# Convolution inputs and half of the pre-normed activations in PSUM, and a smaller fill for two column tiles

## The chip, the cores and the metric

The kernel runs on one core of a Trainium2 chip. The metric is the device time of one execution in microseconds. The core's engines are named as in the profile: PE is TensorE (PEld its weight loads), DVE is VectorE, ACT is ScalarE, POOL is GpSimd, SP the engine that issues most of the weight DMAs. SBUF is the working memory; PSUM is the accumulation memory that the matmuls write, here used as eight banks of 128 x 512 f32.

## What is computed

One inference step of a four-layer decoder trunk with model width 1024, for a prompt of 512 positions and a sample group of 8 sequences with 4 new positions each. Every layer is a token mixer followed by a SwiGLU feed-forward network, each behind an RMS norm and with a residual. Only the second mixer matters here, the Conformer convolution:

```python
z = einsum(h, w_in) + b_in;  a, gate = split(z)
g = a * sigmoid(gate)
ext = concatenate([buf, g])                  # buf: the last 30 rows (zeros for the prompt)
c = depthwise_causal(ext, dw) + dw_b         # 31 taps per channel
c = silu(layernorm(c));  y = einsum(c, w_out)
```

For a sample sequence `ext` has 30 + 4 rows, and each of its four outputs is the sum of 31 products per channel.

## The kernel before

**Tiling.** Channels lie on the 128 partitions; a width of 1024 is NC = 8 column tiles. The positions are two halves: A holds 256 prompt positions, B the other 256 and the 32 sample positions (8 sequences by 4). Every f32 product is three matmuls of split operands (hi by hi, hi by lo, lo by hi). The "hi" copy of weights and activations is an ACT cast, the "lo" part is a subtraction of two SBUF operands on DVE or POOL.

**The order of the work.** `Stream` (L258) holds a list of steps: each has weight loads, matmuls (`mm`, L393, or `mm_pair`, L413) and an evacuation generator. Python writes the program of every engine in order, and each engine runs its own in order. `Timed` (L91) adds up an estimated time for DVE (`dve.t`), POOL and PE while the program is written. Side work, such as the taps of the convolution, is a generator put on a job list; after each step `background` (L287) takes pieces of it until `dve.t` has reached `pe.t - MARGIN[fill]`. `MARGIN` (L1553) is -1.0 for fill 0, 2, 4 and 0.5 for fill 1, 3, 5: with the first, DVE's program is filled to 1.0 us past PE's estimated time, with the second to 0.5 us short of it.

**Weights** come by SP's DMA into four "raw" buffers, are cast by ACT into "hi" and subtracted into "lo"; where `rel` is set, as in the stretch of this case, POOL does most of the "lo" parts (`Load.low`, L171).

**The stages around the change** (us from the span's start): conv_in(A), 224 to 280; ffn(0, B), 280 to 491, with the taps of half A as background; the output projection of A, 491 to 516; conv_in(B), 516 to 572; ffn(1, A), 572 to 774, with the taps of half B, and behind them its layer norm, as background.

**Pre-normed activations.** `Norm.prepare` (L543) multiplies x by gain and 1/rms before the matmuls, for half B of layer 0's FFN (nf0), half B of conv_in (n1) and half A of layer 1's FFN (nf1). For each pair of column tiles DVE writes `hn_` (L552), ACT casts it to `H_h_`, and `split_lo` (L611) subtracts: the odd tile of the pair on DVE, the even one on POOL.

**The convolution.** For each column tile c, `gate_evac` (L1076) makes the sigmoid, `a_evac` (L1104) writes `ce_` (prompt) and `cs_` (sample: 8 x 34 columns, 30 from the state's DMA) and starts the job `conv_taps` (L1157). The job runs 31 taps over 256 prompt positions into two PSUM accumulators `ct0` and `ct1` and then, for half B, the sample positions two at a time: one DVE multiply of overlapping windows of `cs_` by the taps (SBUF by SBUF, 2 x 8 x 31 = 496 elements) into a PSUM tile `cw_`, and one DVE reduce of it to 16 elements. The taps' operand, a slice of `colsT`, has its 31 values 8 f32 apart. `conv_norm` (L1205) follows the last tile.

PSUM tiles all come from one pool of eight (`PS`, L126); a new tile waits for the last use of the tile whose bank it takes. SBUF tiles of this size (`T`, L123) come from a pool of 104.

Of the kernel before, what the change touches and what calls it, by code (L numbers as in the profile page):

```python
# [12 lines left out]
ALU = mybir.AluOpType  # L13
PSUM = bass.MemoryType.PSUM

P = 128
D = 1024
NC = D // P
SEQ = 512
DB, DS = 8, 4  # L20
# [9 lines left out]
CW, SW = 31, 3  # L30
# [8 lines left out]
HP = SEQ // 2  # L39
# [14 lines left out]
C_DW = C_CB + 2 * NC  # L54
# [17 lines left out]
def trunk_kernel(  # L72
# [11 lines left out]
    ap = ctx.enter_context(tc.tile_pool(name="ap", bufs=NBUF))  # L84
# [4 lines left out]
    act = nc.scalar  # L89
# [29 lines left out]
    dve = Timed(nc.vector, operand, 0.00104, 0.07, LEAST)  # L119
# [3 lines left out]
    def T(name, dt=F32):  # L123
        return ap.tile([P, TW], dt, tag="A", name=name)

    def PS(name):  # L126
        return pp.tile([P, 512], F32, tag="ps", name=name)

    def b3(v, n=DB):
        return v.rearrange("p (b l) -> p b l", b=n)  # L130

    x = [cp.tile([P, NC, HW[h]], F32, tag=f"x{h}", name=f"x{h}") for h in (A, B)]
    colsT = cp.tile([P, N_COL], F32, tag="par", name="colsT")
# [9 lines left out]
    def col(i):  # L143
        return colsT[:, i : i + 1]
# [233 lines left out]
    def settle(most=9):  # L378


        t = max(dve.t, pool.t) + SETTLE
        while pe.t < t and most and not S.draining:
            most -= 1
            yield None
# [116 lines left out]
    class Norm:  # L501
# [41 lines left out]
        def prepare(self, h, eng):  # L543
            w, nm = HW[h], f"{self.name}_{h}"
            yield
            out = yield from token_rsqrt(self.acc, (h,), nm, settle(RLAG))
            r = out[h]
            yield
            for c in range(0, NC, 2):
                vs = []  # L550
                for i in (c, c + 1):
                    v = T(f"hn_{nm}_{i}")[:, :w]  # L552
                    dve.scalar_tensor_tensor(
                        v, x[h][:, i, :], gains[:, self.g + i : self.g + i + 1], r[:, :w],
                        op0=ALU.mult, op1=ALU.mult,
                    )
                    self.hs[h][i] = split(v, w, f"h_{nm}_{i}")
                    vs.append(v)
                yield
                for i, v in zip((c, c + 1), vs):  # L560
                    split_lo(self.hs[h][i], v, w, dve if i % 2 else eng)
# [42 lines left out]
    def split(src, w, name):  # L604

        hi = T(f"H_{name}", F32R)
        lo = T(f"L_{name}", F32R)
        act.copy(hi[:, :w], src)  # L608
        return hi, lo

    def split_lo(parts, src, w, eng):  # L611
        hi, lo = parts
        eng.tensor_sub(lo[:, :w], src, hi[:, :w].bitcast(F32))
# [5 lines left out]
    def cols_of(src, name, share, sum=False):  # L619

        return [Load(src[:, i], 1024, f"{name}_{i}", share, sum) for i in range(2)]
# [255 lines left out]
    t = wp.tile([P, 1024], F32, tag="hi", name="ht_0", bufs=AHI + 1)  # L877
# [192 lines left out]
    LS = CB + DS  # L1070

    def conv_in(h, fill):
        w = HW[h]
        sig, exts = {}, {}

        def gate_evac(ps, c):  # L1076
            yield from n1.wait((h,))
            t = sig[c] = T(f"ct_{h}_{c}")
            src = ps[h]
            if h not in n1.pre:  # L1080
                dve.tensor_mul(t[:, :w], ps[h][:, :w], n1.r[h][:, :w])
                src = t
            act.activation(t[:, :w], src[:, :w], AF.Sigmoid, bias=col(C_CB + NC + c))
            yield

        def a_mm(wt, c):
            e = ext[h][c] = T(f"ce_{h}_{c}")
            if h == A:
                pool.memset(e[:, :CB], 0.0)
            else:  # L1090
                pool.tensor_copy(e[:, :CB], cpre[:, c, :])
            if wt:
                return mm(wt, n1.hs, (h,), f"ca_{c}")

        def gate_mm(wt, c, ps=None):
            if h == B:
                for cc in ((0, 1) if c == 0 else (c + 1,)):
                    if cc < NC:
                        exts[cc] = T(f"cs_{cc}")
                        nc.sync.dma_start(exts[cc][:, : DB * LS], st_conv[cc])  # L1100
            ps = ps or mm(wt, n1.hs, (h,), f"cg_{c}")
            return n1.first(ps, (h,)) if c == 0 else ps

        def a_evac(ps, c):  # L1104
            yield from n1.wait((h,))
            e = ext[h][c]
            t = sig.pop(c)
            q = ps[h]
            if h not in n1.pre:
                q = T(f"cq_{h}_{c}")  # L1110
                dve.tensor_mul(q[:, :w], ps[h][:, :w], n1.r[h][:, :w])
            ba = col(C_CB + c)
            ev = None
            if h == B:
                ev = b3(exts[c][:, : DB * LS])
                dve.scalar_tensor_tensor(
                    ev[:, :, CB:], b3(q[:, HP:w]), ba, b3(t[:, HP:w]), op0=ALU.add, op1=ALU.mult
                )
            dve.scalar_tensor_tensor(
                e[:, CB : CB + HP], q[:, :HP], ba, t[:, :HP], op0=ALU.add, op1=ALU.mult  # L1120
            )
            if h == A:
                pool.tensor_copy(cpre[:, c, :], e[:, HP : HP + CB])
            else:
                nc.sync.dma_start(o_cp[:, c, :], e[:, HP : HP + CB])
                nc.sync.dma_start(o_cs[:, c], ev[:, :, DS:])
            S.job(conv_taps(h, c, e, ev))
            if c == NC - 1:
                S.job(conv_norm(h))
            yield  # L1130

        def pair_mm(wt):
            pss = mm_pair((wt[:NC], wt[NC:]), n1.hs, (h,), "cga")
            a_mm(None, 0)
            gate_mm(None, 0, pss[0])
            return pss

        for c in range(NC):
            la, lg = cols_of(w_cin[c], f"ci{c}_{h}", True)
            if c == 0:  # L1140
                S.add([lg, la], pair_mm, lambda pss: both(gate_evac(pss[0], 0), a_evac(pss[1], 0)),
                      flush=True, fill=fill)
                continue
            S.add([lg], lambda wt, c=c: gate_mm(wt, c),
                  lambda ps, c=c: gate_evac(ps, c), flush=(c == 0), fill=fill)
            S.add([la], lambda wt, c=c: a_mm(wt, c), lambda ps, c=c: a_evac(ps, c),
                  fill=fill)

    late = []

    def windows(ev, t):

        v = ev[:, :, t : t + CW]
        p, b, k = v.ap
        return bass.AP(tensor=v.tensor, offset=v.offset, ap=[p, [1, 2], b, k])

    def conv_taps(h, c, e, ev):  # L1157
        w = HW[h]
        cc = cv[h][c] = T(f"cc_{h}_{c}")

        outs = [PS(f"ct{i}_{h}_{c}")[:, :HP] for i in range(2)]
        for k in range(CW):
            o = outs[k % 2]
            wk = col(C_DW + k * NC + c)
            src = e[:, k : k + HP]
            if k == 0:
                dve.tensor_scalar(o, src, wk, col(C_DWB + c), op0=ALU.mult, op1=ALU.add)
            elif k == 1:
                dve.tensor_scalar(o, src, wk, None, op0=ALU.mult)
            else:  # L1170
                dve.scalar_tensor_tensor(
                    cc[:, :HP] if k == CW - 1 else o, src, wk, o, op0=ALU.mult, op1=ALU.add
                )
            if k == 11 and late:
                late.pop()()
            if k % 2:
                yield 0.8
        if ev is not None:

            taps = colsT[:, C_DW + c : C_DW + CW * NC : NC].unsqueeze(1).unsqueeze(1).to_broadcast([P, 2, DB, CW])  # L1180
            for t in range(0, DS, 2):
                pr = PS(f"cw_{c}_{t}")
                pv = pr[:, : 2 * DB * CW].rearrange("p (i b k) -> p i b k", i=2, b=DB)
                dve.tensor_mul(pv, windows(ev, t), taps)
                dve.tensor_reduce(
                    b3(cc[:, HP:w]).rearrange("p b t -> p t b")[:, t : t + 2, :],
                    pv,
                    axis=mybir.AxisListType.X, op=ALU.add,
                )
                yield 1.2  # L1190
            pool.tensor_scalar(cc[:, HP:w], cc[:, HP:w], col(C_DWB + c), None, op0=ALU.add)
        dve.tensor_add(cc[:, :HP], cc[:, :HP], outs[1])

        def gather():

            if c == 0:
                accm[h] = T(f"cm_{h}")
                act.copy(accm[h][:, :w], cc[:, :w])
            else:
                pool.tensor_add(accm[h][:, :w], accm[h][:, :w], cc[:, :w])  # L1200

        late.append(gather)
        yield 0.7
# [291 lines left out]
    for c in range(NC):  # L1495
        lc, lx = cols_of(w_sin[c], f"si{c}", 0)
        S.add([lc], lambda wt, c=c: cg_mm(wt, c),
              lambda ps, c=c: cg_evac(ps, c), flush=(c == 0))
# [175 lines left out]
```

## Time and profile before

| what | us |
|---|---|
| median of 3 runs | 2146.82 |
| lowest, highest of them | 2145.12, 2147.32 |
| the profiled execution, its own time | 2145.55 |
| its span, first to last instruction | 2143.8 |
| mean granted PE clock, share of full speed | 0.993 |

The profile covers one execution. Its busy times say how long an engine executed; a wait row says which engine waited before which operation, for whom, and for how long in total. The time that counts is the median of the runs; the profiled execution is 1.27 us below it.

### The profile page before, as it was taken

Reading aid. Unit: us, or ns where it says so; the run is one execution under the profiler, and the core shown is the slowest. Engines: PE = TensorE matmul, PEld = TensorE weight load, DVE = VectorE, ACT = ScalarE, POOL = GpSimd, SP = SyncE. Lnnn points to the kernel's source line nnn. Section 1 sums busy time; section 2 is a strip of 40 time slices with the busy share of each in tenths; the row PEclk is TensorE's granted clock in tenths of the full one; section 3 lists DMA queues with packets and bytes.
Section 4 is the critical chain, followed back from the end, with each engine's and each line's share of the span. In section 5 each row is a group of like instructions: output and inputs, shape, how many; then the busy total and the mean of one; then the engine's idle time right before and its main releaser. Section 6 shows DMA issues by size and latency. Waiting matters only on the chain.

```text
span 2143.8 us, 42353 instructions
## 1 busy us (share of the span) xinstructions
PE 2107.1 (98%) x16678; PEld 2096.1 (98%) x16678; DVE 1500.7 (70%) x3159; ACT 1017.0 (47%) x1770; POOL 651.4 (30%) x502
## 2 busy tenths in 40 slices
PE   9999999999999999999999999999999999999997
PEld 9999999999999999999999999999999999999997
DVE  8857799616999666566488667686765649585675
ACT  5445543535444654344335646364532246364463
POOL 4011687879788840000043102021000001011121
PEclk9999999999999999999999999999999999999998
DMA  7645555556856564546224746565545555575562
GB/s 270 201 143 168 182 182 148 177 155 181 171 167 187 158 206 152 172 160 179 96 82 141 170 114 153 133 147 145 136 97 87 94 140 109 133 163 126 138 151 72
DMA packets 130191, 320.81 MB, mean 150 GB/s; under 512 B 32557, under 2 KB 40329, under 8 KB 129729
## 3 DMA queue, kind: packets, MB, share of 16 engines
q1 hardware_dynamic: 110664, 279.47, 43.8%
q0 software_dynamic: 18176, 37.33, 10.6%
q8 instruction: 131, 2.15, 0.4%
q10 hardware_dynamic: 1152, 1.32, 0.2%
q14 instruction: 68, 0.55, 0.1%
HBM read 313.81 MB, written 4.62 MB: 149 GB/s over the span
## 4 chain that ended last, share of the span: by engine, by line
PE 84%; DVE 12%; DMA 1%; ACT 1%; issue 1%; SPq 0%; POOL 0%; DVEq 0%; ACTq 0%; POOLq 0%
PE ps_o L109 23%; PE p_w L109 18%; PE ps_g L109 11%; PE ps_u L109 10%; DVE ct L109 4%; PE ps_gv L109 3%; PE ps_go L109 2%; PE ps_sc L109 2%; PE ps_sx L109 2%; PE ps_so L109 2%; PE ps_sbg L109 2%; PE ps_co L109 2%; DVE cw L109 1%; PE ps_gu L109 1%; DMA raw_fi<-in_w_fin 1%; DVE vT L109 1%
## 5 line engine op out<-in xcount | busy, mean ns | idle before, releaser
L109 PE MATMUL ps_o<-H_p,hi_fo 128*128 128x288 f32 (+1 forms) x1408 | 350.2, 288 | 0.1
L109 PE MATMUL ps_o<-L_p,hi_fo 128*128 128x288 f32 (+1 forms) x1408 | 350.0, 288 | 0.1
L109 PE MATMUL ps_o<-H_p,lo_fo 128*128 128x288 f32 (+1 forms) x1408 | 349.5, 288 | 0.0
L169 ACT CAST hi_fi<-raw_fi 128x1024 fp32r<-128x1024 f32 x192 | 200.6, 1047 | 135.0 <-DMA raw_fi<-in_w_fin 48.1
L109 PEld LDWEIGHTS ps_o<-L_p,hi_fo 128*128 128x128 f32 x1408 | 245.8, 188 | 1.2 <-DVE L_p L109 1.2
L109 PEld LDWEIGHTS ps_o<-H_p,hi_fo 128*128 128x128 f32 x1408 | 245.7, 188 | 0.5 <-ACT H_p L608 0.3
L109 PEld LDWEIGHTS ps_o<-H_p,lo_fo 128*128 128x128 f32 x1408 | 245.9, 188 | 0.0
L169 ACT CAST hi_fo<-raw_fo 128x768 fp32r<-128x768 f32 (+2 forms) x194 | 150.2, 775 | 198.6 <-PE ps_o L109 111.1
L249 POOL DMA_DIRECT2D lo_w_a<-in_w_fin x92 | 80.5, 1000 | 444.5 <-ACT lo_w_a L248 425.7
L109 POOL TENSOR_TENSOR lo_fi<-raw_fi,hi_fi 128x1024 fp32r<-128x1024 f32 (+1 forms) x86 | 207.0, 2424 | 23.7 <-PE ps_u L109 7.4
L109 DVE TENSOR_TENSOR lo_fo<-raw_fo,hi_fo 128x768 fp32r<-128x768 f32 (+3 forms) x130 | 113.8, 878 | 122.9 <-issue 64.0
L109 DVE SCALAR_TENSOR_TENSOR ct<-ce,colsT,ct 128x256 f32<-128x256 f32 x448 | 182.2, 480 | 0.0
L109 DVE TENSOR_TENSOR lo_fi<-raw_fi,hi_fi 128x1024 fp32r<-128x1024 f32 (+1 forms) x92 | 114.7, 1249 | 62.5 <-ACT t L735 17.3
L109 PE MATMUL p_w<-L_t_f,hi_w_s 128*128 128x272 f32 x432 | 124.5, 288 | 0.0
L109 PE MATMUL p_w<-H_t_f,lo_w_s 128*128 128x272 f32 x432 | 124.2, 287 | 0.0
L109 PE MATMUL p_w<-H_t_f,hi_w_s 128*128 128x272 f32 x432 | 124.1, 287 | 0.0
L109 PE MATMUL ps_u<-hH_f,hi_fi 128*128 128x256 f32 (+1 forms) x464 | 123.7, 289 | 0.0
L109 PE MATMUL ps_g<-hH_f,hi_fi 128*128 128x256 f32 (+1 forms) x464 | 123.7, 289 | 0.0
L109 PE MATMUL ps_g<-hL_f,hi_fi 128*128 128x256 f32 (+1 forms) x464 | 123.3, 288 | 0.0
L109 PE MATMUL ps_u<-hL_f,hi_fi 128*128 128x256 f32 (+1 forms) x464 | 123.3, 288 | 0.0
L109 PE MATMUL ps_g<-hH_f,lo_fi 128*128 128x256 f32 (+1 forms) x464 | 122.9, 287 | 0.1
L109 PE MATMUL ps_u<-hH_f,lo_fi 128*128 128x256 f32 (+1 forms) x464 | 122.8, 287 | 0.0
(429 smaller groups left out, 6690.8 us busy)
## 6 DMA issues: line engine op xcount, KB each, us to landing
raw_fi<-in_w_fin SPq DMA_DIRECT2D x192, 512.0 KB, 4.3
raw_fo<-in_w_fout SPq DMA_DIRECT2D x96, 384.0 KB, 3.2
raw_w<-in_w_fin SPq DMA_DIRECT2D x72, 512.0 KB, 4.2
raw_fo<-in_w_fout SPq DMA_DIRECT2D x94, 320.0 KB, 3.1
lo_w_a<-in_w_fin POOLq DMA_DIRECT2D x92, 256.0 KB, 5.0
raw_ci<-in_w_cin SPq DMA_DIRECT2D x32, 512.0 KB, 4.3
raw_co<-in_w_cout SPq DMA_DIRECT2D x16, 512.0 KB, 4.8
raw_gi<-in_w_gin SPq DMA_DIRECT2D x16, 512.0 KB, 3.9
```

The lines of the kernel that those rows point to most:

```text
L109: return fn(*a, **k)
L169: act.copy(self.hi, self.raw)
L249: nc.gpsimd.dma_start(self.lo, self.pair.plain(self.k)[1], accum_op=ALU.add)
```

## The change

In `prepare`, the `hn_` tile of every odd column tile is taken from PSUM and not from SBUF. In `conv_taps`, ACT copies the sample's 8 x 34 inputs into a PSUM tile `cw_c` after tap 21; the four positions are then done one at a time, each with a multiply of 248 elements (PSUM by SBUF, result in SBUF) and a reduce to 8 elements. In `conv_in`, the steps of the column tiles 6 and 7 get fill + 1: 1 in place of 0 for half A, 5 in place of 4 for half B.

```diff
@@ Norm.prepare
-                    v = T(f"hn_{nm}_{i}")[:, :w]
+                    v = (PS if i % 2 else T)(f"hn_{nm}_{i}")[:, :w]
@@ conv_in
+            f = fill + int(c + 2 >= NC)
             S.add([lg], lambda wt, c=c: gate_mm(wt, c),
-                  lambda ps, c=c: gate_evac(ps, c), flush=(c == 0), fill=fill)
+                  lambda ps, c=c: gate_evac(ps, c), flush=(c == 0), fill=f)
             S.add([la], lambda wt, c=c: a_mm(wt, c), lambda ps, c=c: a_evac(ps, c),
-                  fill=fill)
+                  fill=f)
@@ conv_taps
+            if k == 21 and ev is not None:
+                ex = b3(PS(f"cw_{c}")[:, : DB * LS])
+                act.copy(ex, ev)
...
-            taps = colsT[...].unsqueeze(1).unsqueeze(1).to_broadcast([P, 2, DB, CW])
-            for t in range(0, DS, 2):
-                pr = PS(f"cw_{c}_{t}")
-                pv = pr[:, : 2 * DB * CW].rearrange("p (i b k) -> p i b k", i=2, b=DB)
-                dve.tensor_mul(pv, windows(ev, t), taps)
+            taps = colsT[...].unsqueeze(1).to_broadcast([P, DB, CW])
+            for t in range(DS):
+                pv = b3(T(f"cw_{c}_{t}")[:, : DB * CW])
+                dve.tensor_mul(pv, ex[:, :, t : t + CW], taps)
                 dve.tensor_reduce(
-                    b3(cc[:, HP:w]).rearrange("p b t -> p t b")[:, t : t + 2, :],
-                    pv,
-                    axis=mybir.AxisListType.X, op=ALU.add,
+                    b3(cc[:, HP:w])[:, :, t : t + 1], pv, axis=mybir.AxisListType.X, op=ALU.add
                 )
-                yield 1.2
+                yield 0.7
```

## Rows read from the trace of the kernel before

**Rows 1.** The page, busy time of each engine over the span.
```profile
span 2143.8 us, 42353 instructions
...
PE 2107.1 (98%) x16678; PEld 2096.1 (98%) x16678; DVE 1500.7 (70%) x3159; ACT 1017.0 (47%) x1770; POOL 651.4 (30%) x502
```

**Rows 2.** Windows: stretch, length, busy PE, PEld, DVE, ACT, POOL, clock, DMA, GB/s.
```profile
516.00:572.00 56.00, 51.72 (x391) 51.34 (x390) 52.99 (x110) 25.68 (x39) 44.05 (x33) 1.00 0.79 172
572.00:640.00 68.00, 63.28 (x497) 62.73 (x498) 67.02 (x139) 27.90 (x42) 53.68 (x27) 0.92 0.56 165
640.00:720.00 80.00, 78.09 (x653) 77.19 (x652) 70.83 (x147) 36.03 (x55) 70.97 (x44) 1.00 0.54 171
```

**Rows 3.** Timeline of PE, matmuls after a wait: start, us, [idle before, releaser].
```profile
552.76 0.37 PE L109 MATMUL ps_ca<-H_h_n,hi_ci 128*128 128x288 f32 x1 [1.49 <-DVE cc L109]
...
571.92 0.36 PE L109 MATMUL ps_gu<-H_h_f,hi_fi 128*128 128x256 f32 x1 [2.79 <-DVE ce L109]
...
611.51 0.39 PE L109 MATMUL ps_u<-H_h_f,hi_fi 128*128 128x256 f32 x1 [0.89 <-DVE L_p L109]
618.36 0.55 PE L109 MATMUL ps_g<-H_h_f,hi_fi 128*128 128x256 f32 x1 [3.74 <-DVE cc L109]
...
681.88 0.39 PE L109 MATMUL ps_g<-H_h_f,lo_fi 128*128 128x256 f32 x1 [1.14 <-POOL lo_fi L109]
```

**Rows 4.** Windows around two of those waits, columns as before.
```profile
572.00:576.00 4.00, 4.00 (x21) 4.00 (x22) 3.96 (x8) 1.04 (x1) 0.00 (x0) 0.57 1.11 294
...
616.00:620.00 4.00, 1.64 (x8) 1.67 (x9) 3.93 (x5) 1.42 (x3) 0.59 (x1) 0.59 0.71 242
620.00:630.00 10.00, 10.00 (x73) 10.00 (x72) 10.00 (x27) 4.46 (x8) 8.68 (x6) 0.82 0.30 92
630.00:640.00 10.00, 10.00 (x87) 10.00 (x86) 9.93 (x20) 4.09 (x8) 8.77 (x4) 1.00 0.49 132
```

**Rows 5.** Timeline of DVE, 557 to 619: start, us, instruction.
```profile
557.44 2.66 DVE L109 TENSOR_TENSOR L_h_f<-hn_f,H_h_f 128x256 fp32r<-128x256 f32 x1
...
573.65 1.08 DVE L109 TENSOR_TENSOR cw<-cs,colsT 128x496 f32<-128x496 f32 x1
574.77 0.68 DVE L109 TENSOR_REDUCE cc<-cw 128x16 f32<-128x496 f32 x1
575.36 1.11 DVE L109 TENSOR_TENSOR cw<-cs,colsT 128x496 f32<-128x496 f32 x1
...
613.33 4.17 DVE L109 TENSOR_TENSOR cw<-cs,colsT 128x496 f32<-128x496 f32 x1
```

**Rows 6.** Timeline of POOL, same stretch; in brackets the idle time before.
```profile
557.43 2.38 POOL L109 TENSOR_TENSOR lo_ci<-raw_ci,hi_ci 128x1024 fp32r<-128x1024 f32 x1
...
577.28 0.36 POOL L109 TENSOR_SCALAR cc<-cc,colsT 128x32 f32<-128x32 f32 x1 [7.38 <-DVE cc L109]
...
604.82 11.77 POOL L109 TENSOR_TENSOR lo_fi<-raw_fi,hi_fi 128x1024 fp32r<-128x1024 f32 x5
```

**Rows 7.** Groups by line and form, DVE: busy us, mean ns, then idle before.
```profile
L109 DVE SCALAR_TENSOR_TENSOR ct<-ce,colsT,ct 128x256 f32<-128x256 f32 x448 | 182.2, 480 | 0.0
...
L109 DVE TENSOR_TENSOR lo_w_s<-ss_w_s,hi_w_s 128x512 fp32r<-128x512 f32 x128 | 83.0, 685 | 34.0 <-PE ps_o L109 28.3 <-PE p_w L109 4.7 <-ACT H_t_f L608 1.0
...
L109 DVE TENSOR_TENSOR cw<-cs,colsT 128x496 f32<-128x496 f32 x16 | 30.6, 1910 | 0.0
...
L109 DVE TENSOR_TENSOR q_A<-c_w,c_w 128x256 f32<-128x256 f32 x36 | 15.1, 419 | 0.0
...
L109 DVE TENSOR_TENSOR t<-ps_g,r_f 128x256 f32<-128x256 f32 x29 | 12.1, 417 | 10.0 <-ACT r_f L460 10.0
...
L109 DVE TENSOR_TENSOR L_h_f<-hn_f,H_h_f 128x256 fp32r<-128x256 f32 x4 | 7.5, 1876 | 0.0
```

**Rows 8.** Timeline of ACT, the one copy of a convolution tile.
```profile
560.52 0.43 ACT L1198 COPY cm<-cc 128x288 f32<-128x288 f32 x1 [2.59 <-DVE cc L109]
```

**Rows 9.** Waits of ACT from 572 to 702: total us, times, longest.
```profile
ACT hi_fi L169 <- DMA raw_fi<-in_w_fin: 22.2, 14, 5.5
```

More of the change, by code (lines that the diff above doesn't have):

```diff
@@ L1143, in conv_in @@
                 continue
+            f = fill + int(c + 2 >= NC)
             S.add([lg], lambda wt, c=c: gate_mm(wt, c),
-                  lambda ps, c=c: gate_evac(ps, c), flush=(c == 0), fill=fill)
+                  lambda ps, c=c: gate_evac(ps, c), flush=(c == 0), fill=f)
             S.add([la], lambda wt, c=c: a_mm(wt, c), lambda ps, c=c: a_evac(ps, c),
-                  fill=fill)
+                  fill=f)
     late = []
[L1151 to L1155, printed above, removed]
     def conv_taps(h, c, e, ev):
@@ L1178, in conv_taps @@
         if ev is not None:
-            taps = colsT[:, C_DW + c : C_DW + CW * NC : NC].unsqueeze(1).unsqueeze(1).to_broadcast([P, 2, DB, CW])
-            for t in range(0, DS, 2):
-                pr = PS(f"cw_{c}_{t}")
-                pv = pr[:, : 2 * DB * CW].rearrange("p (i b k) -> p i b k", i=2, b=DB)
-                dve.tensor_mul(pv, windows(ev, t), taps)
+            taps = colsT[:, C_DW + c : C_DW + CW * NC : NC].unsqueeze(1).to_broadcast([P, DB, CW])
+            for t in range(DS):
+                pv = b3(T(f"cw_{c}_{t}")[:, : DB * CW])
+                dve.tensor_mul(pv, ex[:, :, t : t + CW], taps)
                 dve.tensor_reduce(
-                    b3(cc[:, HP:w]).rearrange("p b t -> p t b")[:, t : t + 2, :],
-                    pv,
-                    axis=mybir.AxisListType.X, op=ALU.add,
+                    b3(cc[:, HP:w])[:, :, t : t + 1], pv, axis=mybir.AxisListType.X, op=ALU.add
                 )
-                yield 1.2
+                yield 0.7
             pool.tensor_scalar(cc[:, HP:w], cc[:, HP:w], col(C_DWB + c), None, op0=ALU.add)
```

## The prediction

> **What bounds the kernel now.** I read four views in turn. The page's busy times come first: PE is busy for 2107.1 us of a span of 2143.8 [rows 1], so a change that removes no matmul can win only from PE's 36.7 idle us and from any time at a lower clock. Windows by stage say where these lie: conv_in(B) and the part of ffn(1, A) that has half B's taps as background [rows 2]. From 516 to 720 PE idles 4.28 + 4.72 + 1.91 = 10.91 us, DVE is busy for 190.8 of 204 us, and one stretch was granted 0.92 of the full clock. PE's timeline names the cause: four waits on DVE between 551 and 619, of 1.49, 2.79, 0.89 and 3.74 us, **8.9** together [rows 3]. Two are for the sample's reduce, which frees a PSUM bank, one for a late `ce_`, one for a late `L_p`.
>
> The clock adds to this. [...] At 8.7 matmuls per us the three stretches lack 13.8, 6.3 and 14, or 34 matmuls of 0.115 us: **3.9 us**. So what DVE's lateness costs PE there is 8.9 + 3.9 = **12.8 us**.
>
> Why is DVE late? The same multiply of 496 elements takes 1.08 us at 573.65 and 4.17 at 613.33 [rows 5]. At the first, POOL had been idle for the 7.38 us up to 577.28; at the second, POOL ran five `lo_fi` in a row up to 604.82 + 11.77 = 616.59 [rows 6]. The multiply ended at 617.50, about its own 1.08 us after POOL stopped. The subtraction `L_h_f` at 557.44 ended at 560.10, just after POOL's `lo_ci` (557.43 + 2.38 = 559.81). Both read two SBUF operands. The taps, with one operand in SBUF and one in PSUM, average 480 ns over 448 through the same stretches; `L_h_f` averages 1876 for 256 elements, where a subtraction or product of two SBUF operands without POOL beside it takes 419 [rows 7]. So DVE's operations with two SBUF operands wait for POOL, and those with one do not.
>
> **The change, part by part.**
>
> *`hn_` in PSUM.* The odd `L_h_f` then reads one operand from PSUM. Four of them cost 7.5 us now; at the 417 ns of a product from PSUM [rows 7] they cost 1.7: DVE saves **5.8 us**, all before conv_in(B) ends at 572. The same edit in the preparations of nf0 and n1 lies ahead of every wait of rows 3, under matmuls that do not stop; I take 0 there, and without that cover it would be a gain. Writing `hn_` to PSUM costs 0: the taps also read SBUF and write PSUM, at 480 ns [rows 7]; the operations of this size in these rows lie between 417 and 480 ns whichever memory they write, so four writes move DVE by under 0.3 us either way.
>
> [...] The rows show 417 ns from PSUM and 419 from SBUF at 256 elements [rows 7], no extra; measurement decides.
>
> *The sample's positions.* Now, per column tile, two multiplies of 1.91 us on average [rows 7], each with a reduce: 0.04 from the multiply's end to the reduce (573.65 + 1.08 to 574.77), 0.59 from the reduce's start to the next multiply [rows 5]. That is 2 x 2.54 = 5.08 us. Afterwards there are four pairs. No row has the multiply of 248 elements with one operand in PSUM. From below: 0.41, like the 256-element product from PSUM. From above: 1.08, as if half the elements saved nothing. Two-operand forms of 256 and 512 elements take 419 and 685 ns, so 0.15 is fixed; 1.08 for 496 is dearer than either, and the taps' operand keeps its step of 8 values, so I halve only the rest: 0.15 + 0.93/2 = **0.62**. The reduce likewise: 0.15 + 0.53/2 = 0.42, of which 0.33 counts before the next start. A position costs 0.62 + 0.04 + 0.33 = 0.99, a tile 3.96, against 5.08: 1.1 less, **9.0 us** over eight tiles. With the lower price a tile is 3.1 and the saving 15.7; with the upper (0.59 a reduce too) it is 6.8 and DVE loses 14.
>
> [...]
>
> *ACT's copy of the inputs.* Eight copies of 272 elements; the nearest row is 0.43 us for 288 [rows 8], so 3.4 us on an engine that is busy 27.9 of 68 us [rows 2]. From SBUF to PSUM no row shows one; as an added instruction it can't gain, and at twice the row it is 7 us of idle ACT. It is issued ten taps (over 4 us) before its reader, so I take 0 for DVE; without that cover its wait would count, see the third rival.
>
> *Fill.* The steps of column tiles 6 and 7 fill DVE to 0.5 us short of PE and not 1.0 past it: 1.5 us, three or four taps, move behind the last evacuations of conv_in, into ffn(1, A). DVE's total does not change. The late `ce_` that PE waits 2.79 us for comes some 1.5 us sooner from this alone. For half A the same edit moves taps where PE shows no wait on DVE: 0; its cover is ffn(0, B), over 200 us long. No DMA moves; SP's queue only sees `ce_` earlier.
>
> *The sum.* DVE saves 5.8 + 9.0 = 14.8 us on a nearly gapless queue; PE's losses to it are 12.8, so PE becomes the bound again. By position: `L_h_f`'s 5.8 and the fill come before 572, where 1.49 + 2.79 = 4.3 are needed; the rest must come from the sample's multiplies, of which the 4.17 us one stands right ahead of the wait that ends at 618.36, with nothing to spare. I keep 1.3 us for what remains there, and leave the 1.14 us wait on POOL's `lo_fi`, which is late next. Forecast: 12.8 - 1.3 = **11.5 us** off. On the profiled execution's 2145.55 that is 2134.05; it stood 1.27 below the median, so I predict **2135.3** against 2146.82.
>
> **Rivals.**
>
> *Banks (slower).* During nf1's preparation the eight banks hold the broadcast of 1/rms, an `hn_`, `ct0`, `ct1`, now the sample's inputs for ten taps and four positions, and the matmul tiles of this step and the last: seven. A matmul then reuses the bank that DVE released last, and PE waits at each tile as it did for 1.49 and 3.74 us [rows 3]. For: two of today's waits are just such releases. Against: a bank released one step back is early enough if DVE is on time, and its lateness shrinks by 14.8 us. It decides once the waits lose more than 12.8 + 4.3 = 17.1 us, 2.1 per column tile; at 2.6 a tile the time is about 2155.
>
> *POOL or the transfers take over.* POOL is busy 168.7 of 204 us [rows 2]; take 12.8 away and it is 88%. PE already waited 1.14 us for a `lo_fi`, and DMA was busy 0.79 in conv_in(B). Five such waits leave 11.5 - 5.7 = 5.8 us of gain: 2141. Against: POOL also loses the multiplies that block it.
>
> *ACT late with the copy.* ACT runs in order, and `hi_fi` waits for its DMA, 14 times, up to 5.5 us [rows 9]. The cover is about 4 us, so the worst case costs 5.5 - 4 = 1.5 us and the copy itself 0.43; three in eight would cost 5.8 and leave 5.7: 2141.1.
>
> *No effect.* If the multiply still waited for POOL with one operand in PSUM, four waits would replace two, each 1.91 - 1.08 = 0.83: DVE would pay 4 x 1.82 = 7.3 a tile for 5.1, and the 5.8 of `L_h_f` would not come: 18 us more on DVE, up to 2165. The steady 480 ns of the taps speak against it. A milder form, where the gain goes into other waits altogether, leaves 2145 to 2148.
>
> **How the numbers follow.** Forecast 0.58; POOL, transfers or ACT taking part of it 0.24; no change 0.11; slower 0.07 (banks 0.05, still waiting 0.02). A measurement of this kernel can tell 0.2%, 4.3 us. Faster is 0.58 + 0.24 = 0.82, same 0.11, slower 0.07. The range holds the first two cases: its low end takes all 10.9 idle us, the 3.9 of clock and the 1.7 by which the lowest run lies under the median (16.5: 2130.3), its high end is a gain of 4.3: 2142.5. The lower price of the multiply changes nothing, as PE bounds; the upper lies with the slower cases.
>
> **What would show it.** Right: four multiplies a tile near 0.62 us with little spread, `L_h_f` on DVE near 0.42, no PE wait on `cc_` or `ce_` above 1 us between 516 and 720, full clock in 572 to 640, and ffn(1, A) ending some 12 us earlier, with all behind it moved alike. Wrong: multiplies above 1 us or spread like today's, new PE waits on `L_h_f`, on the multiply or on ACT's copy, DVE waiting on ACT before a multiply, or a larger wait on `lo_fi`.

## The result, and the profile after

The changed kernel takes 2138.6 us (median of 6 runs, 2134.92 to 2139.12), the kernel before 2147.07 beside it (6 runs): a ratio of 0.995 [0.9938, 0.9961], faster by more than the 0.2% that can be told apart. The forecast was 2135.3.

The page of the changed kernel, its span and busy times, against [rows 1]:

```profile
span 2137.2 us, 42390 instructions
...
PE 2107.3 (99%) x16678; PEld 2097.1 (98%) x16678; DVE 1485.7 (70%) x3191; ACT 1018.5 (48%) x1778; POOL 646.2 (30%) x502
```

PE's busy time is the same to 0.2 us, and the span is 6.6 us shorter. The equal busy time hides differences that cancel: 4.9 us less for the matmuls of the stage measured below, 3.9 us more for those ahead of it, with the start of this execution, which ran at a low clock (0.54 granted from 10 to 20 us, last section), and 1.2 us more for those behind it. The same three stretches as in [rows 2], of the changed kernel:

```profile
516.00:572.00 56.00, 54.42 (x417) 54.19 (x417) 49.68 (x122) 28.48 (x46) 45.53 (x34) 1.00 0.84 186
572.00:640.00 68.00, 67.78 (x573) 67.61 (x572) 64.02 (x160) 31.86 (x50) 58.25 (x33) 1.00 0.71 181
640.00:720.00 80.00, 78.38 (x659) 77.64 (x658) 67.57 (x156) 37.47 (x58) 70.25 (x43) 1.00 0.57 179
```

PE's idle time in these 204 us falls from 10.91 to 1.58 + 0.22 + 1.62 = 3.42 us, the granted clock is 1.00 in all three, and 572 to 640 holds 573 matmuls where there were 497. (In these fixed windows the changed kernel's work begins 5.7 us later; the two marks below take that out.) DVE's busy time falls by 9.6 us to 181.3. What PE still waits for there, from the table of waits (total us, times, longest):

```profile
PE ps_cg L109 <- ACT ct L1083: 1.6, 1, 1.6
PE ps_o L109 <- POOL lo_fo L109: 1.4, 1, 1.4
PE ps_g L109 <- DVE cc L109: 0.2, 1, 0.2
PE ps_g L109 <- POOL lo_fi L109: 0.2, 1, 0.2
```

Of the four waits on DVE of [rows 3], 8.9 us together, 0.2 is left. Two waits are new: one on `lo_fo` of POOL, and one of 1.58 us on ACT's `ct`, which frees a PSUM bank.

The operations whose prices the prediction had to estimate, by tile (min/median/max in ns, first and last start in us):

```profile
L109 DVE TENSOR_TENSOR cw<-cw,colsT x32: 614/641/685, 553.9 to 695.7; 128x248 f32<-128x248 f32 x32
L109 DVE TENSOR_REDUCE cc<-cw x32: 412/414/416, 554.6 to 696.4; 128x8 f32<-128x248 f32 x32
L1173 ACT COPY cw<-cs x8: 380/391/397, 539.3 to 686.2; 128x272 f32<-128x272 f32 x8
```

The multiply with one operand in PSUM spreads over 71 ns; with both in SBUF its average was 1910 and one took 4.17 us [rows 5, 7]. The clearest single place is DVE's timeline under a row of five `lo_fi` on POOL; first DVE, then POOL, both of the changed kernel:

```profile
614.61 0.64 DVE L109 TENSOR_TENSOR cw<-cw,colsT 128x248 f32<-128x248 f32 x1
615.28 0.41 DVE L109 TENSOR_REDUCE cc<-cw 128x8 f32<-128x248 f32 x1
615.61 0.62 DVE L109 TENSOR_TENSOR cw<-cw,colsT 128x248 f32<-128x248 f32 x1
```

```profile
603.75 11.86 POOL L109 TENSOR_TENSOR lo_fi<-raw_fi,hi_fi 128x1024 fp32r<-128x1024 f32 x5
```

POOL is busy until 615.61. The first multiply starts and ends inside that, at the ordinary 0.64 us; before, the one in this place ended only after POOL did [rows 5, 6].

**Where the 8.5 us are.** The work that the edit touches lies between two marks: the first matmul of conv_in(A), and the first matmul of the stage that follows the two ffn passes (`ps_gv`). By tile, the first start on each row is the mark; first the kernel before, then the changed one:

```profile
L109 PE MATMUL ps_cga<-hH_n,hi_ci x16: 274/282/385, 231.3 to 237.7; 128*128 128x256 f32 x16
...
L109 PE MATMUL ps_gv<-hH_n,hi_gi x256: 277/293/387, 1010.9 to 1121.2; 128*128 128x256 f32 x128
```

```profile
L109 PE MATMUL ps_cga<-hH_n,hi_ci x16: 274/282/386, 237.0 to 243.4; 128*128 128x256 f32 x16
...
L109 PE MATMUL ps_gv<-hH_n,hi_gi x256: 278/293/560, 1004.1 to 1114.6; 128*128 128x256 f32 x128
```

Before: 1010.9 - 231.3 = 779.6 us. After: 1004.1 - 237.0 = 767.1 us, **12.5 less**. What comes behind takes 1132.9 and 1133.1 us. What comes ahead took 5.7 us longer in this profiled execution, though nothing is edited there: 5.7 - 12.5 + 0.2 = -6.6, the difference of the spans. PE between the two marks, columns as in [rows 2], first the kernel before, then the changed one:

```profile
231.30:1010.90 779.60, 766.50 (x5971) 763.26 (x5970) 555.40 (x1114) 371.47 (x563) 455.05 (x271) 0.99 0.57 170
```

```profile
237.00:1004.10 767.10, 761.62 (x5970) 759.26 (x5969) 540.23 (x1146) 373.16 (x571) 449.23 (x271) 1.00 0.59 173
```

PE's idle time falls from 13.10 to 5.48 us, by 7.6, and its busy time for the same matmuls (to one) by 4.9: together the 12.5. This distance between the marks, called the stage below, is the finer measure of each edit; the start is taken up in the last section.

### The profile page after: what moved, and what is told of

Read it like the earlier page. It is cut to its first block, busy times and chain, and to the rows that moved or that the text cites. A ratio compares the mean times of both kernels' runs of the same rounds, so it can differ in the third digit from the quotient of the medians.

```text
span 2137.2 us, 42390 instructions
## 1 busy us (share of the span) xinstructions
PE 2107.3 (99%) x16678; PEld 2097.1 (98%) x16678; DVE 1485.7 (70%) x3191; ACT 1018.5 (48%) x1778; POOL 646.2 (30%) x502
## 4 chain that ended last, share of the span: by engine, by line
PE 88%; DVE 7%; ACT 2%; DMA 2%; issue 1%; POOL 0%; ACTq 0%; DVEq 0%; POOLq 0%
PE ps_o L109 24%; PE p_w L109 18%; PE ps_g L109 12%; PE ps_u L109 12%; PE ps_gv L109 3%; PE ps_co L109 2%; PE ps_sx L109 2%; PE ps_sc L109 2%; PE ps_sbg L109 2%; PE ps_so L109 2%; PE ps_cg L109 2%; PE ps_ca L109 1%; DVE ct L109 1%; DMA raw_fi<-in_w_fin 1%; PE ps_go L109 1%; PE pd L109 1%
```

## Experiments

The theory to test: DVE was late because its operations with two SBUF operands waited for POOL; one operand in PSUM ends that; PE then bounds, and gives back at most what it lost. Rivals: the split into single positions does it, or the later taps, or the price of the multiply is set by something else. Each edit is against the kernel named with it.

**1. `hn_` alone** (kernel before plus):

```diff
-                    v = T(f"hn_{nm}_{i}")[:, :w]
+                    v = (PS if i % 2 else T)(f"hn_{nm}_{i}")[:, :w]
```

> Only the odd hn tiles in PSUM; sample taps and fill as before. Theory 1 (a DVE operation with two SBUF operands waits until POOL's operation ends, one with an operand in PSUM does not): L_h_f on DVE falls from 1.88 us mean to 0.42 to 0.45, DVE gains 5.8 us ahead of 572, PE's waits of 1.49 and 2.79 us and the slow clock after them vanish (5.9 us); the 4.17 us multiply and PE's 3.74 us wait at 618 stay in some form. About 4 to 7 us faster than before. Theory 2 (PSUM banks become scarce and PE waits for them): new PE waits in conv_in(B) of over 2 us, no gain.

Measured: 2145.3 us, ratio 0.9985 [0.9972, 0.9997]; stage 1005.7 - 232.0 = 773.7, 5.9 shorter. By tile, and the three largest of PE's waits from 516 to 720:

```profile
L109 DVE TENSOR_TENSOR L_h_f<-hn_f,H_h_f x8: 408/426/450, 169.1 to 555.8; 128x288 fp32r<-128x288 f32 x4, 128x256 fp32r<-128x256 f32 x4
...
L109 DVE TENSOR_TENSOR cw<-cs,colsT x16: 1136/1846/2640, 548.7 to 691.8; 128x496 f32<-128x496 f32 x16
```

```profile
PE ps_g L109 <- POOL lo_fi L109: 1.8, 2, 1.4
PE ps_ca L109 <- DVE ce L109: 1.5, 1, 1.5
PE ps_g L109 <- DVE cc L109: 1.5, 1, 1.5
```

`L_h_f`, up to 2.66 us before, is now at most 0.45, and the untouched multiply still goes up to 2.64: the stall goes with the operand, not with the time or the place. Both waits on DVE ahead of 572 are gone, as expected, but a new one of 1.5 us on `ce` stands in conv_in(B). The stage follows, the whole time barely.

**2. The sample's taps alone** (changed kernel, `hn_` and fill put back):

```diff
-                    v = (PS if i % 2 else T)(f"hn_{nm}_{i}")[:, :w]
+                    v = T(f"hn_{nm}_{i}")[:, :w]
...
-            f = fill + int(c + 2 >= NC)
...
-                  lambda ps, c=c: gate_evac(ps, c), flush=(c == 0), fill=f)
+                  lambda ps, c=c: gate_evac(ps, c), flush=(c == 0), fill=fill)
...
-                  fill=f)
+                  fill=fill)
```

> Only the sample's taps changed (ACT copy to PSUM, four multiplies per tile); hn and fill as before. Theory 1: multiplies 0.61 to 0.69 us with no spread, the wait of 3.74 us at 618 and the clock loss after it vanish, the waits of 1.5 and 2.8 us ahead of 572 stay, since L_h_f keeps its 1.88 us. About 5 to 8 us faster than before. Theory 2 (banks): PE waits on bank releases stay above 3 us in all between 572 and 640.

Measured: 2140.68 us, ratio 0.9962 [0.9948, 0.9975]; stage 1005.9 - 237.8 = 768.1, 11.5 shorter. By tile, and PE's waits from 516 to 640:

```profile
L109 DVE TENSOR_TENSOR L_h_f<-hn_f,H_h_f x8: 415/444/2660, 174.9 to 562.6; 128x288 fp32r<-128x288 f32 x4, 128x256 fp32r<-128x256 f32 x4
```

```profile
PE ps_g L109 <- POOL lo_fi L109: 0.9, 1, 0.9
PE ps_ca L109 <- ACT ct L1083: 0.6, 1, 0.6
PE ps_u L109 <- DVE L_p L109: 0.5, 1, 0.5
```

This part alone brings nearly all of the stage's gain. The waits of 1.49 and 2.79 us ahead of 572 are gone although `L_h_f` still takes up to 2.66 us, which I had not expected. For the first there is a reason in the diff: the product of the multiply lay in PSUM before and lies in SBUF now, so a reduce no longer frees a PSUM bank. For the second, see the last section.

**3. The fill alone** (kernel before plus):

```diff
+            f = fill + int(c + 2 >= NC)
             S.add([lg], lambda wt, c=c: gate_mm(wt, c),
-                  lambda ps, c=c: gate_evac(ps, c), flush=(c == 0), fill=fill)
+                  lambda ps, c=c: gate_evac(ps, c), flush=(c == 0), fill=f)
...
-                  fill=fill)
+                  fill=f)
```

> Only the fill of column tiles 6 and 7. By my sum three or four taps move behind the last evacuations: PE's 2.79 us wait at 572 falls to about 1.3, DVE's total work is as before and its lateness shows up at 618 instead. 0 to 2 us faster than before. Rival: nothing moves, the wait at 572 stays at 2.8.

Measured: 2148.24 us, ratio 0.9994 [0.9983, 1.0005]; stage 1013.0 - 236.8 = 776.2, 3.4 shorter. PE's waits on DVE from 516 to 720:

```profile
PE ps_u L109 <- DVE cc L109: 1.9, 2, 1.7
PE ps_ca L109 <- DVE cc L109: 1.6, 1, 1.6
...
PE ps_g L109 <- DVE cc L109: 0.8, 1, 0.8
```

The 2.79 us wait on `ce` is gone, DVE's lateness shows in three waits on `cc`, and in the time no difference can be told. The three parts alone give 5.9 + 11.5 + 3.4 = 20.8 us of stage, all together 12.5: they pay for the same waits.

**4. Four positions, inputs left in SBUF** (changed kernel with):

```diff
-                ex = b3(PS(f"cw_{c}")[:, : DB * LS])
-                act.copy(ex, ev)
+                ex = ev
```

> The changed kernel, but its four multiplies read the sample's inputs from SBUF, with no ACT copy: the split into four alone. Theory 1: each multiply waits for POOL again, mean 1.2 to 1.7 us and up to 3 us and more; DVE loses 2 to 4 us per tile against the changed kernel, PE waits of several us return between 572 and 640; 8 to 20 us slower than the changed kernel, level with the kernel before or slower. Rival (the smaller pieces are what helps): multiplies stay near 0.64 us and the time is that of the changed kernel.

Measured: 2152.45 us, ratio 1.0016 [1.0004, 1.0028]; stage 1013.8 - 232.5 = 781.3, which is 14.2 longer than in the changed kernel and 1.7 longer than before. By tile, and the largest of PE's waits from 516 to 720:

```profile
L109 DVE TENSOR_TENSOR cw<-cs,colsT x32: 616/703/2442, 549.4 to 703.2; 128x248 f32<-128x248 f32 x32
```

```profile
PE cmean L109 <- POOL cm L109: 3.2, 1, 3.2
PE ps_u L109 <- POOL lo_fi L109: 2.8, 2, 1.7
PE ps_o L109 <- ACT H_p L608: 2.2, 1, 2.2
```

Same instructions, same shapes, same minimum (616 and 614 ns); only the operand's place differs, and single multiplies are again held, up to 2.44 us. Their mean is 1.09 us, less than the 1.2 to 1.7 expected. Without the operand in PSUM the split brings nothing: with the other two parts in, the stage is no shorter than before. (The ratio is within the 0.2% that can't be told.)

That it is POOL that holds them shows when each multiply is laid beside POOL's timeline. Here two of DVE and, behind them, POOL:

```profile
613.13 1.45 DVE L109 TENSOR_TENSOR cw<-cs,colsT 128x248 f32<-128x248 f32 x1
...
614.94 0.64 DVE L109 TENSOR_TENSOR cw<-cs,colsT 128x248 f32<-128x248 f32 x1
```

```profile
602.23 11.85 POOL L109 TENSOR_TENSOR lo_fi<-raw_fi,hi_fi 128x1024 fp32r<-128x1024 f32 x5
```

POOL is busy until 614.08. Of the 32 multiplies, the 16 with no POOL operation beside them take 0.62 to 0.65 us, the 16 with one 0.75 to 2.44. In the kernel before, the three without one take 1.08 to 1.11 us, the 13 others 1.15 to 4.17. In the changed kernel, with the operand in PSUM, it makes no difference: 21 beside POOL take 0.61 to 0.69 us, 11 alone 0.62 to 0.67.

The lateness comes out in other waits: PE's rows name POOL and ACT, which are late in turn.

**5. Two positions at a time, from PSUM** (changed kernel with):

```diff
...
-            for t in range(DS):
-                pv = b3(T(f"cw_{c}_{t}")[:, : DB * CW])
-                dve.tensor_mul(pv, ex[:, :, t : t + CW], taps)
+            for t in range(0, DS, 2):
+                pr = PS(f"cw_{c}_{t}")
+                pv = pr[:, : 2 * DB * CW].rearrange("p (i b k) -> p i b k", i=2, b=DB)
+                dve.tensor_mul(pv, windows(ex, t), taps)
...
-                yield 0.7
+                yield 1.2
```

> The changed kernel with ACT's copy to PSUM kept, but the positions two at a time as before: a multiply of 496 elements from PSUM. Theory 1 (the operand's memory decides): multiplies near 1.08 us with no spread, 3.4 us of DVE a tile against the changed kernel's 4.0; PE already bounds, so the stretch from the first matmul of conv_in(A) to the first of the spatial gating layer (779.6 us before, 767.1 in the changed kernel) stays within 2 us of 767. Rival (the split is needed): multiplies spread up to 2 us and more, and the stretch is 4 us longer or more.

Measured: 2137.61 us, ratio 0.9953 [0.9937, 0.9968]; stage 996.8 - 231.6 = 765.2. By tile:

```profile
L109 DVE TENSOR_TENSOR cw<-cw,colsT x16: 1103/1144/1182, 548.4 to 683.7; 128x496 f32<-128x496 f32 x16
```

All 16 multiplies within 79 ns, near the 1.08 that this form took beside an idle POOL [rows 5], and the time of the changed kernel. With 4, this settles it: the place of the operand is what matters, the number of positions is not. Nor is the place of the product: it lies in PSUM in the kernel before and here, in SBUF in 4 and in the changed kernel, and in each pair one is held and one is not.

**6. The taps packed.** ACT copies the tile's taps, which lie 8 values apart, side by side (changed kernel with):

```diff
                 act.copy(ex, ev)
+                tp = T(f"tp_{c}")
+                act.copy(tp[:, :CW], colsT[:, C_DW + c : C_DW + CW * NC : NC])
...
-            taps = colsT[:, C_DW + c : C_DW + CW * NC : NC].unsqueeze(1).to_broadcast([P, DB, CW])
+            taps = tp[:, :CW].unsqueeze(1).to_broadcast([P, DB, CW])
```

> The changed kernel with each tile's 31 taps first copied by ACT into neighbouring columns, so that the multiply reads both operands without a step. If the step of 8 f32 is what makes it dear: multiplies fall from 0.64 to about 0.41 us, DVE gains 7 us in all, and the time hardly moves (0 to 2 us faster), because PE bounds. If the price is that of the shape: they stay at 0.64.

Measured: 2135.15 us, ratio 0.994 [0.9925, 0.9954]; stage 1000.5 - 236.2 = 764.3. By tile:

```profile
L109 DVE TENSOR_TENSOR cw<-cw,tp x32: 401/406/421, 553.0 to 691.7; 128x248 f32<-128x248 f32 x32
```

Same count, same memories: 641 ns with the step, 406 without. The step of the taps is what makes this multiply dearer than other products of its size (417 and 419 ns for 256 elements [rows 7]). It is the lowest median of the study, 2.8 us less in the stage than the changed kernel; but the two kernels' intervals overlap.

**7. The input's bank held longer.** ACT copies 20 taps earlier (changed kernel with):

```diff
-            if k == 21 and ev is not None:
+            if k == 1 and ev is not None:
```

> The changed kernel with ACT's copy after tap 1 instead of tap 21, so that its PSUM bank is held for 20 taps (8 us of DVE) longer in every tile. If banks are nearly scarce: PE waits for DVE or ACT above 1 us appear several times between 516 and 720, 3 to 10 us slower than the changed kernel. If one bank more or less does not matter: within 2 us of it.

Measured: 2137.9 us, ratio 0.9954 [0.9937, 0.9971]; stage 999.6 - 232.6 = 767.0. PE's waits from 516 to 640:

```profile
PE ps_g L109 <- DVE cw L109: 1.6, 1, 1.6
PE ps_cg L109 <- ACT ct L1083: 1.6, 1, 1.6
```

One new wait for a bank, of 1.6 us on `cw`, and a stage of the same length; not the several that scarce banks would give. Banks can be felt here, but are far from the 17.1 us that the rival needed.

**8. Squares of the norms in PSUM too.** The `sq_n` additions, of the norm ahead of conv_in(A) among them, are another DVE operation with two SBUF operands (changed kernel with):

```diff
-        def square(self, h, c):
+        def square(self, h, c, psum=False):
...
-            q = self.sq[h, c] = T(f"sq_{self.name}_{h}_{c}")
+            q = self.sq[h, c] = (PS if psum else T)(f"sq_{self.name}_{h}_{c}")
...
-            n.square(h, c)
+            n.square(h, c, eng is dve and c > 0)
```

> The changed kernel, with the squares that DVE adds up (where it is DVE that adds) also in PSUM, so that these additions no longer read two SBUF operands. Theory 1: the additions at 226 to 237 us that last 2.5 us fall to 0.42, PE's 1.0 us wait on hH_n ahead of conv_in(A) shrinks or goes; 1 to 3 us faster than the changed kernel. Rival: hL_n, which has two SBUF operands still, takes over the wait for POOL, and nothing is gained.

Measured: 2138.39 us, ratio 0.9952 [0.9936, 0.9967]; stage 1000.4 - 233.2 = 767.2. DVE's groups by form (busy us, mean ns, idle before), first of the changed kernel, then of this one:

```profile
L109 DVE SCALAR_TENSOR_TENSOR hL_n<-x,colsT,hH_n 128x256 fp32r<-128x256 f32 x24 | 17.7, 736 | 12.8 <-ACT hH_n L530 12.8
...
L109 DVE TENSOR_TENSOR sq_n<-sq_n,sq_n 128x256 f32<-128x256 f32 x14 | 10.3, 733 | 0.0
```

```profile
L109 DVE SCALAR_TENSOR_TENSOR hL_n<-x,colsT,hH_n 128x256 fp32r<-128x256 f32 x24 | 17.9, 745 | 14.7 <-ACT hH_n L530 14.7
...
L109 DVE TENSOR_TENSOR sq_n<-sq_n,sq_n 128x256 f32<-128x256 f32 x14 | 5.8, 413 | 0.0
```

The remedy works on the third kind of operation as well, 733 to 413 ns and 4.5 us off DVE, and wins nothing that can be told. PE's wait of 1.1 us on `hH_n` at the start of conv_in(A), which the changed kernel has, is gone as expected, but the stage is no shorter. `hL_n` did not take the hold over (736 to 745 ns); DVE idles 1.9 us longer for ACT's `hH_n`.

**9. Two positions and packed taps** (the edits of 5 and 6 together).

> Both variants that took DVE time away from the changed kernel together: positions two at a time from PSUM, taps packed. Multiplies of 496 elements at about 0.68 us, 2.7 us of DVE a tile against 4.0. If PE is the bound, nothing more is won than either brought alone: the stretch from the first matmul of conv_in(A) to the first of the spatial gating layer (764.3 us with packed taps, 765.2 two at a time, 767.1 in the changed kernel) within 1 us of 764. If DVE still set something: 762 or less.

Measured: 2135.73 us (5 runs), ratio 0.9944 [0.993, 0.9959]; stage 1004.3 - 238.2 = 766.1. By tile, and the window of 516 to 720:

```profile
L109 DVE TENSOR_TENSOR cw<-cw,tp x16: 669/672/676, 555.1 to 689.0; 128x496 f32<-128x496 f32 x16
```

```profile
516.00:720.00 204.00, 202.02 (x1649) 201.27 (x1649) 171.95 (x414) 100.45 (x162) 177.40 (x112) 1.00 0.68 185
```

The 16 multiplies cost 10.8 us where the changed kernel's 32 cost 20.5. DVE is 9.3 us less busy here than after the change, and PE only 1.4 us more. The stage of 766.1 is longer than the 763 to 765 expected and far from the 762 that a bounding DVE would have given. PE bounds this stretch, and a still faster DVE brings nothing that can be told.

**10. The changed kernel once more**, unaltered.

> The changed kernel once more, unaltered, beside the same runs of the kernel before as the last one. The profiles of the kernel before and of the changed one differ by 12.5 us in that stretch, the medians by 8.5; the first 96 us took about 5 us longer in the one profiled execution of the changed kernel, and in two of the four single-edit kernels, which have the same program there. If that start is chance: ratio near 0.9943 (12 us) to 0.995, and this profile may show the short start. If it belongs to the change: long start again, ratio 0.996.

Measured: 2138.99 us (6 runs), ratio 0.9952 [0.9935, 0.997]; stage 1005.9 - 239.9 = 766.0, 13.6 shorter than before. The start was the long one again, and the ratio lies between the two that were expected, so this run does not decide between chance and the change. Two profiles of one program thus differ by 1.1 us in the stage; differences of that size between kernels above say nothing, and with a single pair the scatter may be larger.

## Why the prediction was right

*What DVE's lateness cost PE: 12.8.* The stage became 12.5 and 13.6 us shorter, at full clock. By parts, between the two marks of the profiled execution: 7.6 us of idle time, where 8.9 - 1.3 = 7.6 were forecast, and 4.9 us of busy time for the same matmuls, where the lower clock was put at 3.9. So the idle time came out as summed, and the clock term was 1.0 us too small if all of that busy time is the clock's. The 3.9 is an estimate from the matmul counts of [rows 4], where the three stretches that lack 13.8, 6.3 and 14 are 572 to 576, the 1.64 busy us from 616 to 620, and 620 to 630, against the 8.7 per us from 630 to 640; no run shows it as a time of its own; what the runs show in its place is the 4.9, at a granted clock of 1.00 after the change and 0.99 before.

*The reason, two SBUF operands beside POOL.* The operand's part is shown three ways: `L_h_f` (1), four positions from SBUF (4) and two from PSUM (5). POOL's part is shown by the traces: in (4), a multiply takes longer than 0.65 us exactly when a POOL operation runs beside it. The longest took 2442 ns there, against 685 in the changed kernel, where 21 also ran beside POOL. No run took POOL's work away, and why a POOL operation holds such a multiply was not shown.

*`hn_`: `L_h_f` to 0.42, 5.8 us off DVE.* In the first experiment, with this edit alone, no `L_h_f` took over 0.45 us, and the stage shortened by 5.9. The `ce` that PE had waited 2.79 us for came 4.6 us sooner.

*No surcharge for PSUM.* With its operand in PSUM, the packed multiply of 248 elements takes 406 ns (6), under the 419 that a product of 256 took from SBUF [rows 7], and the additions of (8), of 256 elements, took 413 ns on average with an operand in PSUM.

*The multiply 0.62 (between 0.41 and 1.08), the reduce 0.42.* Measured 0.64 and 0.41. The argument, that the step of the taps is charged per element, is shown by (6), where the packed multiply falls to the lower bound: packing takes off 235 ns at 248 elements and 1144 - 672 = 472 ns at 496 (5, 9).

*ACT's copy 0.43, at no cost.* Measured 0.39; nothing of DVE waits for it (idle before the multiply: 0.0), and moving it 20 taps forward left the stage as it was (7).

*The fill: total unchanged, `ce` 1.5 us sooner.* The `ce` that PE had waited for, of column tile 6, did come 1.7 us sooner (575.10 is 338.3 after the first mark, against 571.30 or 340.0 before). **The effect on PE was sized too small:** the whole 2.79 us wait went and not 1.5 of it, since this edit also changed which bank the waiting matmul takes (last section). Alone it took 3.4 us off the stage. In the time as a whole its 0.9994 can't be told from nothing, and it isn't needed: (2) does without it.

*The sum by position.* **This step failed in its detail.** It had `L_h_f` and the fill pay the waits before 572, and the multiplies the rest "with nothing to spare". In (1), `L_h_f` alone does pay the larger. But experiment 2 pays for both without either, and (3) pays the larger with the fill alone: each edit also changes the order in which PSUM tiles are taken, and with it where lateness is felt, and that was not in the sum. The total came out because PE bounds it: the multiplies alone gave 11.5 of the 12.5, and the other two parts had little left to pay for.

*What is left, 1.3 us, and POOL next.* The size came out (1.3 and the 2.0 us of waits on others, against 3.4), not the kind: of waits on DVE 0.2 us is left, and ACT and POOL took the rest. From 516 to 720 PE still waits about 1.6 for ACT's `ct`, 1.4 for `lo_fo`, 0.2 for `lo_fi` where 1.14 was left alone. The wait on `ct` is the mechanism of the rival *Banks* at a small price: it stands at 1.5 to 1.6 us in the changed kernel and in 5 to 10, which all hold `hn_` and the inputs in PSUM, and at 0.6 in 2, where `hn_` is in SBUF. In the built program of the changed kernel, the `ps_cg` that waits has the bank of the `ps_cg` of the column tile just before it.

*11.5 us, 2135.3.* The gain was 12.5 in the stage, and 8.5 between the medians; by the interval of the ratio it is 8.4 to 13.3 us, which holds 11.5. Between the profiled executions the difference lies ahead of the first mark: the start was 5.7 us longer in that of the changed kernel. That the medians differ by less than the stage for the same reason is likely, but not shown, since the other runs have no trace.

*Rivals.* POOL took 1.6 us instead of 5.7, and the transfers made ACT no later: its `hi_fi` waited 17.8 us for DMA in 12 waits up to 3.4, against 22.2 and 5.5 [rows 9]. *No effect* is refuted by the multiply's 685 ns at most.

## What to carry to other kernels

When DVE's operations spread widely in time while POOL is busy, look for those with two SBUF operands; putting one operand in PSUM made each of them steady here (the multiply at most 685 ns where it took up to 2442 from SBUF, `L_h_f` at most 450 in (1) where it took up to 2659 before), with no surcharge (413 ns for an addition of 256 elements in (8), 419 for a product of 256 from SBUF). Each such tile takes a bank, though, and changes which bank later tiles get. Work out what PE lost before adding up what DVE saves: three edits that gave 5.9, 11.5 and 3.4 us alone gave 12.5 together. Compare distances between two marks of the traces where whole times scatter by more than the effect.

## What was not expected of the hardware

**The start varies by 5 us.** The first matmul of conv_in(A) starts at 231.3 to 233.2 us in six profiles and at 236.2 to 239.9 in six others. The window of 10 to 20 us, in the kernel before, in the changed kernel and in experiment 7, which has the same program there as the changed kernel:

```profile
10.00:20.00 10.00, 9.72 (x84) 9.72 (x85) 8.75 (x21) 9.18 (x23) 7.40 (x10) 1.00 0.85 325
```

```profile
10.00:20.00 10.00, 8.90 (x42) 8.90 (x42) 5.65 (x18) 5.68 (x14) 3.77 (x6) 0.54 0.68 270
```

```profile
10.00:20.00 10.00, 9.08 (x79) 9.08 (x80) 8.64 (x22) 9.32 (x22) 6.87 (x9) 1.00 0.80 315
```

At a granted 0.54, PE gets through half the matmuls, 42 against 84 and 79. The 40 warm-up matmuls ahead of it, first of the changed kernel, then of experiment 7:

```profile
L109 PE MATMUL warm<-ones x40: 274/275/582, 1.1 to 7.0; 128*128 128x128 f32 x40
```

```profile
L109 PE MATMUL warm<-ones x40: 275/421/583, 1.1 to 8.1; 128*128 128x128 f32 x40
```

In the long starts the warm-up itself came sooner to its full pace (median 275 to 326 ns, against 399 to 421 in the short ones) and was over sooner (its last matmul starts at 7.0 to 7.7 us, against 7.8 to 8.5); PE then waited 2.5 to 3.9 us for the first `pd` (1.6 to 2.6 in the short ones) and went on at the low clock (0.54 to 0.66 granted from 10 to 20 us, against 1.00). The changed kernel had the long start in both its profiles. Its 12 runs also lie in two groups, four from 2133.74 to 2135.22 us with a mean clock of 0.995 or 0.996 and eight from 2137.76 to 2141.16 with 0.992 to 0.995, so I take the start for chance; that it has nothing to do with the change isn't shown, as those runs have no trace.

**Which bank a matmul gets decides whether DVE's lateness reaches PE.** ffn(1, A) begins with two matmuls into a first accumulator `ps_gu`; the third opens a second one. In the kernel before, this third matmul waited 2.79 us for the `ce` of column tile 6, which reads the `ps_ca` tile in the same bank. That `ce` in the kernel before and in experiment 2, from DVE's timeline:

```profile
571.30 0.47 DVE L109 SCALAR_TENSOR_TENSOR ce<-ps_ca,colsT,ct 128x256 f32<-128x256 f32 x1
```

```profile
575.67 0.47 DVE L109 SCALAR_TENSOR_TENSOR ce<-ps_ca,colsT,ct 128x256 f32<-128x256 f32 x1
```

In experiment 2 the third matmul ran at 574.66, 1.0 us before this `ce` started, and did not wait; in experiment 3 at 574.31, 0.8 us before its `ce` at 575.10, and did not wait either. So lateness alone does not make the wait. No row names banks, but the programs built from the kernels do: the second `ps_gu` has the bank of tile 6's `ps_ca` in the kernel before and in experiment 1, and that of tile 6's `ps_cg`, which ACT reads, in 2, in 3 and in the changed kernel. In experiment 1, with the bank as before, PE did not wait because `ce` came in time: at 567.38, 2.4 us ahead of the first `ps_gu` matmul. In the changed kernel it came at 569.02, 8.0 us sooner after the first mark than before, so there the bank no longer mattered.
